# Value projections of 512 columns, and merge gates moved into the attention heads, in a hybrid encoder block

## The chip, the cores and the metric

The kernel runs on one core of a Trainium2 chip. A core has a matrix engine (TensorE, PE in the profile), a vector engine (VectorE, DVE), a scalar engine for activations (ScalarE, ACT), a general engine (GpSimd, POOL) and a queue engine that issues transfers (SyncE, SP). Each runs its own list of instructions in order and waits on semaphores for the others. PE writes to PSUM banks (128 partitions x 512 float32); the other data sits in on-chip SBUF tiles.

The metric is the device time of one execution in microseconds (us), the median of several runs. The profile comes from one further execution; its span runs from the first to the last profiled instruction, and the device time of that execution is a little longer.

## The reference

One block for 512 positions of 1024 features, in float32:

```
u = rmsnorm(x) @ w_in        # columns q | k | v | rnn_x | rnn_gate | gate_A | gate_B, 1024 each
A = chunked_band_attention(q, k, v, rel_table)      # 16 heads x 64, chunks of 64, each with 8 chunks before it
B = rg_lru(conv4(rnn_x)) * gelu(rnn_gate)           # recurrence, 16 block-diagonal gates
gA, gB = sigmoid([gate_A, gate_B] + b_merge)
h = x + (gA * (A @ w_attn_out) + gB * (B @ w_rnn_out)) @ w_o
h = h + (silu(rmsnorm(h) @ w_g) * (rmsnorm(h) @ w_u)) @ w_ffn_out
out = rmsnorm(h)
```

With 512 positions the band of 9 chunks covers every earlier position, so attention is causal by chunk, with a bias per head that depends on the distance (clipped at 128) and a softmax over the keys.

## The kernel before

**Products.** Every large product is made of three matmuls on a rounded high part and a remainder of each operand (`mm3`, lines 76 to 78). The splitting into the two parts (`split`, lines 82 and 83) takes one ScalarE copy for the high part and one VectorE subtraction for the remainder; weights are split the same way after they are loaded. A projection tile is 8 blocks of features x 3 = 24 matmuls into one PSUM bank.

**Weights.** `plan` writes down the order in which weights are used; each has 1024 rows and some columns, loaded as tiles of 512 KB (tag `raw`, three buffers, issued by SP at line 152) and split into tiles tagged `whl` (four buffers of 8 KB a partition in the pool `wp`). `weights(name, ahead)` asks, through `prefetch`, for the named weight and `ahead` further ones. `homes` names another pool for the split tiles of some weights: `v1` to `v3` go to `big` buffers of the pool `rnp`, which the results of the recurrence and later the attention outputs share, and one of them to the later home of two gate tiles.

**Order.** The instructions are put in order when the kernel is built, by a scheduler that walks a simulated time line and takes the program's order as priority; each engine then runs its fixed list. On PE the order inside the attention heads is the program's own (`manual_schedule`).

**First stage** (lines 578 to 588): for four pairs of feature tiles, the projections `xr`, `gr` (recurrent input and its gate), for the first two pairs also `ga` (gate of the attention branch, tiles 0 to 3), and `gb`. Beside them VectorE, ScalarE and GpSimd do the convolution, the GELU, the gates and the scan.

**Between** (lines 629 to 738): queries and keys of the first pair of heads (`q_tile(0)`, `k_tile(0)`), the first four value tiles, and eight tiles `po_yb` of `B @ w_rnn_out`, with the scores of head 0 among them.

**Heads** (lines 739 to 749): for each head h, PE runs in this order: transposes of the probabilities of h (`pT`, line 682), scores of h+1 (`s`, lines 663 and 664), the tiles that `laid(h)` puts before the weighted sum, the weighted sum of h (`o`, line 702), and the tiles that `laid(h)` puts after it. Between the scores of a head and its transposes lies a chain on the other engines: VectorE adds the bias and takes the maximum (line 667), ScalarE takes the exponential with its sum (668), VectorE the reciprocal (669), and GpSimd multiplies (671). `laid` puts `q_tile` or `k_tile` before the sum of heads 0 to 12, one value tile of 256 columns (four heads) behind heads 0 to 11, and the gate tiles 4 to 7 behind head 12 and before the sums of heads 13 to 15. The bias of a head is a broadcast load of 256 KB (`bias_tile`, two buffers, issued by SP at line 430), followed by a `memset` of one corner on GpSimd.

**After** the heads: `ya` = A @ w_attn_out, merge, `w_o`, the feed-forward part and the last norm; the change does not touch them.

Of the kernel before, what the change touches and what calls it, by code (L numbers as in the profile page):

```python
# [8 lines left out]
F32 = mybir.dt.float32  # L9
# [27 lines left out]
def block_kernel(ctx: ExitStack, tc: tile.TileContext, x, norm_mix_g, w_in, b_merge, rel_table,  # L37
# [62 lines left out]
    for j in range(0, KT, 2):  # L100
        plan(f"xr{j}", cols(w_in, C_XR + j * P))
        plan(f"gr{j}", cols(w_in, C_GR + j * P))
        if j < 4:
            plan(f"ga{j}", cols(w_in, C_GA + j * P))
        plan(f"gb{j}", cols(w_in, C_GB + j * P))

    def plan_qk(pr):
        plan(f"qk{pr}", cols(w_in, C_Q + pr * P, P), cols(w_in, C_K + pr * P, P))

    def plan_v(gr):  # L110
        plan(f"v{gr}", cols(w_in, C_V + gr * CW))

    plan_qk(0)
    plan_v(0)
    for j in range(0, KT, 2):
        plan(f"yb{j}", cols(w_rnn_out, j * P))
    for pr in range(1, HEADS // 2):
        plan_qk(pr)
        if pr in (1, 3, 5):
            plan_v((pr + 1) // 2)  # L120
    for j in (4, 6):
        plan(f"ga{j}", cols(w_in, C_GA + j * P))
    for j in range(0, KT, 2):
        plan(f"ya{j}", cols(w_attn_out, j * P))
    for cc in range(2):
# [94 lines left out]
    def prefetch(n):  # L220
        while len(made) < min(n, len(chunks), index.get(barrier[0], len(chunks))):
            name, parts, rows, kts = chunks[len(made)]
            if name in strassen:
                made.append(weight_sums(name))
                continue
            tiles = []
            wide = sum(width for *_, width in parts)
            step = 4 * CW // wide
            for k in range(0, kts, step):
                n_ = min(step, kts - k)  # L230
                if (name, k) in homes:
                    pl, tag, bufs = homes[name, k]
                    hl = pl.tile([P, 2, n_, wide], F32R, tag=tag, bufs=bufs, name=f"whl_{name}_{k}")
                elif name in extra:
                    hl = extra[name].tile([P, 2, n_, wide], F32R, tag="whl", bufs=4, name=f"whl_{name}_{k}")
                else:
                    hl = wp.tile([P, 2, n_, wide], F32R, tag="whl", bufs=4, name=f"whl_{name}_{k}")
                if (name, k) not in raws:
                    load(name, k)
                raw = raws.pop((name, k))  # L240
                if len(made) == 0 and k:
                    act.activation(hl[:, 0], raw[:], AF.Copy)
                    pool.tensor_sub(hl[:, 1], raw[:], f(hl[:, 0]))
                else:
                    split(hl[:, 0], hl[:, 1], raw[:])
                tiles.append(hl)
            made.append(lambda part, k, at, tiles=tiles, step=step: tiles[k // step][:, part, k % step, at])

    def weights(name, ahead=1):
        prefetch(index[name] + 1 + ahead)  # L250
# [175 lines left out]
    def bias_tile(h):  # L426
        b = aw.tile([P, S], F32, tag="bias", bufs=2, name=f"bias{h}")
        src = ext_d[h:h + 1, 0:S]
        band = bass.AP(tensor=src.tensor, offset=src.offset, ap=[[1, P], [1, S]])
        sp.dma_start(out=b[:], in_=band)  # L430
        pool.memset(b[64:128, 448:512], NEG)
        return b

# [131 lines left out]
        return po  # L565


    zs = [[zp.tile([P, 2, S], F32, name=f"z{w}{j}") for j in range(0, KT // (1 + (w == "a")), 2)] for w in "ab"]
    ta, zB = ([t[j // 2][:, j % 2] for j in range(2 * len(t))] for t in zs)
    for gr in (1, 2, 3):  # L570
        for k in (0, 4):
            homes[f"v{gr}", k] = (zp, "late", 1) if (gr, k) == (3, 4) else (rnp, "big", 4)

    def gate(w, j):
        po = tile_of(f"g{'ab'[w]}{j - j % 2}", j % 2)
# [3 lines left out]
    for j in range(0, KT, 2):  # L579
        for c in range(2):  # L580
            conv[j + c] = rnn_conv(j + c, tile_of(f"xr{j}", c, ahead=2))
        for c in range(2):
            po = tile_of(f"gr{j}", c, "mm" if j == 0 else "t")
            conv[j + c] += (rnn_gelu(j + c, po),)
            gates_of(j + c)
        for w in range(j // 4, 2):
            for c in range(2):
                gate(w, j + c)


    rg_stack.close()
# [44 lines left out]

    vs = {}

    def v_tile(gr, t):
        wv = weights(f"v{gr}")  # L640
        po = mm_tile(f"po_v{gr}_{t}", "mm" if gr else "t")
        for k in range(KT):
            mm3(po[:, 0:256], xnT[k][:, 0, t * P:(t + 1) * P], xnT[k][:, 1, t * P:(t + 1) * P],
                wv(0, k, whole), wv(1, k, whole), k == 0, k == KT - 1)
        v = aw.tile([P, 2, 4, HD], F32R, tag="v", bufs=8, name=f"v{gr}_{t}")
        split(v[:, :, 0::3], v[:, :, 1:3], po[:, 0:256].rearrange("p (a b d) -> p a b d", a=2, b=2))
        vs.setdefault(gr, []).append(v)


    def scores(h):  # L650
        pr, e = divmod(h, 2)
        q, kh, kl = qk[pr]
        bias = bias_tile(h)
        lsum = cp.tile([P, NT], F32, tag="lsum", bufs=2, name=f"l{h}")
        nmax = cp.tile([P, NT], F32, tag="nmax", bufs=2, name=f"m{h}")
        rl = cp.tile([P, NT], F32, tag="rl", bufs=2, name=f"rl{h}")
        prob = [aw2.tile([P, (qb + 1) * P], F32, tag=f"p{qb}", name=f"p{h}_{qb}") for qb in range(NT)]
        banks = [ss.tile([P, S], F32, tag="s", bufs=2, name=f"s{h}_{i}") for i in range(2)] + [mm_tile(f"s{h}_2")]
        scs = [banks[0][:, 0:P], banks[0][:, P:3 * P], banks[1][:, 0:3 * P], banks[2][:]]
        for qb in range(NT):  # L660
            w = (qb + 1) * P
            qs = q[:, e, qb * P:(qb + 1) * P]
            pe.matmul(scs[qb], qs, kh[:, e, 0:w], start=True, stop=False)
            pe.matmul(scs[qb], qs, kl[:, e, 0:w], start=False, stop=True)
        for qb in range(NT):
            w = (qb + 1) * P
            dve.tensor_tensor_reduce(prob[qb][:], scs[qb], bias[:, S - w:S], -1.0, 3e38, ALU.add, ALU.min, nmax[:, qb:qb + 1])  # L667
            act.activation(prob[qb][:], prob[qb][:], AF.Exp, bias=nmax[:, qb:qb + 1], scale=-1.0, accum_out=lsum[:, qb:qb + 1])  # L668
        dve.reciprocal(rl[:], lsum[:])  # L669
        for qb in range(NT):  # L670
            pool.tensor_scalar(prob[qb][:], prob[qb][:], rl[:, qb:qb + 1], 1.0, ALU.mult, ALU.mult)  # L671
        return prob
# [18 lines left out]
    def weigh(h, pp):  # L691
        pr, e = divmod(h, 2)
        own, other = halves(e)
        if e == 0:
            oacc.append(tg_.tile([P, S], F32, tag="tg", name=f"oacc{pr}"))
        acc = oacc[pr]
        po = mm_tile(f"o{h}")
        for kb in range(NT):
            i, lo, n = ((0, 0, 512), (1, 0, 384), (2, 0, 256), (2, 256, 128))[kb]
            st = vs[pr // 2][kb][:, pr % 2, 2 * e:2 * e + 2].rearrange("p a d -> p (a d)")  # L700
            for part in range(2):
                pe.matmul(po[:, S - n:S], st, pp[i][:, part, lo:lo + n], start=kb == 0 and part == 0, stop=kb == NT - 1 and part == 1)  # L702
        act.activation(acc[own, :], po[other, :], AF.Copy)
        dve.tensor_add(acc[own, :], po[own, :], acc[own, :])
        if e == 1:
            if pr % 2 == 0:
                aT_pairs.append(rnp.tile([P, 2, 2, S], F32R, tag="big", bufs=4, name=f"aT{pr}"))
            o = aT_pairs[-1][:, pr % 2]
            split(blocks(o[:, 0]), blocks(o[:, 1]), backwards(acc[:]))
            aT.append(o)  # L710

    def laid(h):
        before, after = [], []
        if h == 0:
            before += [lambda: q_tile(1), lambda: k_tile(1)]
        elif h < 13:
            before.append(lambda: (q_tile if h % 2 else k_tile)(1 + (h + 1) // 2 if h % 2 else 1 + h // 2))
        if h < 12:  # L720
            after.append(lambda: v_tile(1 + h // 4, h % 4))
        if h == 12:
            late = zp.tile([P, 2, 2, S], F32, tag="late", bufs=1, name="za_late")
            ta.extend(late[:, i, c] for i in range(2) for c in range(2))
            after.append(lambda: gate(0, 4))
        elif h > 12:
            before.append(lambda: gate(0, h - 8))
        return before, after

    for t in range(NT):  # L730
        v_tile(0, t)
# [7 lines left out]
    with tc.manual_schedule(engines={mybir.EngineType.PE}):  # L739
        for h in range(HEADS):  # L740
            pp = transposed(h, prob)
            if h + 1 < HEADS:
                prob = scores(h + 1)
            before, after = laid(h)
            for what in before:
                what()
            weigh(h, pp)
            for what in after:
                what()
    aw2_stack.close()  # L750
    wo_stack, wop = opened("wo", 4)
    extra["wo1"] = wop
# [253 lines left out]
```

## Time and profile before

| | us |
|---|---|
| device time, three runs | 878.87, 879.03, 879.04 (median 879.03) |
| device time of the profiled execution | 878.95 |
| its span | 877.2 |
| mean granted clock of TensorE | 0.998 |

In the rows of a time line the first number is the start in us from the span's start, the second the duration in us, then engine, line, operation, tile written <- tiles read, shape and count; a bracket gives the idle time of the engine just before, and what ended it. Durations of matmuls overlap, since they are pipelined: what a matmul costs is the distance to the next one's start. The list of issues shows a transfer's queue (SPq, ACTq), size and time to landing.

### The profile page before, as it was taken

What the parts mean: (1) busy time and instruction counts of PE and PEld (TensorE: products, weight loads), DVE (VectorE), ACT (ScalarE), POOL (GpSimd) and SP (SyncE); (2) the same over time, 40 slices, a digit from 0 to 9 for tenths busy, and PEclk for the clock granted to TensorE, in tenths of its full rate; (3) what the DMA queues carried; (4) which work ended last, traced back from release to release, by engine and by line L of the source; (5) the groups of instructions that cost most, each with busy time, mean ns of one, the idle gap of its engine ahead of it and who ended that gap; (6) DMA issues with size and microseconds to landing.
All of it is one profiled execution on the core that took longest, in us unless ns stands there. A gap on an engine that the chain in (4) does not pass through costs nothing.

```text
span 877.2 us, 13330 instructions
## 1 busy us (share of the span) xinstructions
PE 868.0 (99%) x5220; PEld 770.6 (88%) x5220; DVE 544.0 (62%) x858; ACT 483.6 (55%) x838; POOL 105.8 (12%) x138
## 2 busy tenths in 40 slices
PE   8999999999999999999999999999999999999997
PEld 6977888788888899998888889999999999888886
DVE  5776557563466676665556557888888886554203
ACT  6586757752367676666534367555555555723103
POOL 2013112120112232333100000000000001301100
PEclk9999999999999999999999999999999999999999
DMA  8323323333343233222224530433333332353002
GB/s 269 97 78 98 98 87 97 121 96 96 108 138 91 74 93 88 72 73 61 88 85 148 207 96 28 142 101 117 98 103 102 118 112 74 134 177 120 26 1 97
DMA packets 86080, 90.11 MB, mean 103 GB/s; under 512 B 5376, under 2 KB 74608, under 8 KB 86016
## 3 DMA queue, kind: packets, MB, share of 16 engines
q1 hardware_dynamic: 84640, 85.78, 31.5%
q10 hardware_dynamic: 1376, 3.47, 1.0%
q8 instruction: 41, 0.67, 0.3%
q14 instruction: 23, 0.19, 0.1%
HBM read 87.10 MB, written 2.14 MB: 102 GB/s over the span
## 4 chain that ended last, share of the span: by engine, by line
PE 97%; ACT 1%; DVE 1%; DMA 0%; issue 0%; ACTq 0%
PE po_out L76 5%; PE po_out L77 5%; PE po_out L78 5%; PE p_fg L76 2%; PE o L702 2%; PE p_fg L78 2%; PE p_fu L78 2%; PE p_fg L77 2%; PE p_fu L77 2%; PE p_fu L76 2%; PE pT L682 2%; PE po_v L76 2%; PE po_v L78 2%; PE po_v L77 2%; PE po_gb L77 2%; PE po_ga L76 2%
## 5 line engine op out<-in xcount | busy, mean ns | idle before, releaser
L77 PE MATMUL po_out<-whl_fo,act_hi 128*128 128x512 f32 (+1 forms) x198 | 72.5, 366 | 0.0
L76 PE MATMUL po_out<-whl_fo,act_hi 128*128 128x512 f32 (+1 forms) x198 | 72.3, 366 | 0.0
L78 PE MATMUL po_out<-whl_fo,act_lo 128*128 128x512 f32 (+1 forms) x198 | 71.7, 365 | 0.0
L83 DVE TENSOR_TENSOR whl_fo<-raw_fo,whl_fo 128x1024 fp32r<-128x1024 f32 x22 | 27.9, 1274 | 44.2 <-ACT whl_fo L82 43.8
L671 POOL TENSOR_SCALAR p<-p,rl 128x128 f32<-128x128 f32 (+1 forms) x64 | 39.6, 638 | 127.6 <-DVE rl L669 127.3
L82 ACT ACTIVATE whl_fo<-raw_fo 128x1024 fp32r<-128x1024 f32 x22 | 23.1, 1058 | 48.8 <-PE po_out L78 35.2
L890 POOL TENSOR_TENSOR act_lo<-act,act_hi 128x1024 fp32r<-128x1024 f32 x4 | 10.9, 2717 | 323.5 <-ACT act_hi L889 321.5
L668 ACT ACTIVATE p<-p,m 128x128 f32<-128x128 f32 (+1 forms) x64 | 35.8, 560 | 16.2 <-DVE m L667 16.2
L78 PEld LDWEIGHTS po_out<-whl_fo,act_lo 128*128 128x128 f32 x198 | 37.3, 189 | 6.0
L76 PEld LDWEIGHTS po_out<-whl_fo,act_hi 128*128 128x128 f32 x198 | 37.4, 189 | 6.0
L77 PEld LDWEIGHTS po_out<-whl_fo,act_hi 128*128 128x128 f32 x198 | 37.4, 189 | 5.8
L76 PE MATMUL po_v<-whl_v,xnT 128*128 128x256 f32 x128 | 36.8, 287 | 0.0
L78 PE MATMUL po_v<-whl_v,xnT 128*128 128x256 f32 x128 | 36.2, 283 | 0.0
L77 PE MATMUL po_v<-whl_v,xnT 128*128 128x256 f32 x128 | 36.2, 283 | 0.0
L83 DVE TENSOR_TENSOR pp<-pT,pp 128x384 fp32r<-128x384 f32 (+1 forms) x48 | 27.8, 597 | 8.5 <-ACT pp L82 8.5
L667 DVE CUSTOM_DVE_ANT_0 p<-s,bias 128x128 f32<-128x128 f32 (+1 forms) x64 | 29.1, 484 | 0.0
L76 PE MATMUL po_gr<-xnT,whl_gr 128*128 128x512 f32 (+1 forms) x80 | 28.2, 354 | 0.1
L83 DVE TENSOR_TENSOR whl_qk<-raw_qk,whl_qk 128x1024 fp32r<-128x1024 f32 x16 | 21.2, 1326 | 11.0 <-ACT whl_qk L82 11.0
L83 DVE TENSOR_TENSOR whl_fg_s<-s_fg,whl_fg_s 128x1024 fp32r<-128x1024 f32 x20 | 25.6, 1294 | 3.7 <-ACT whl_fg_s L82 3.7
L77 PE MATMUL po_xr<-xnT,whl_xr 128*128 128x512 f32 (+1 forms) x80 | 27.8, 353 | 0.0
L77 PE MATMUL po_gr<-xnT,whl_gr 128*128 128x512 f32 (+1 forms) x80 | 27.6, 346 | 0.0
L78 PE MATMUL po_gr<-xnT,whl_gr 128*128 128x512 f32 (+1 forms) x80 | 27.5, 348 | 0.0
(340 smaller groups left out, 3027.8 us busy)
## 6 DMA issues: line engine op xcount, KB each, us to landing
raw_fg<-in_w_ffn_in_dram SPq DMA_DIRECT2D x24, 512.0 KB, 4.2
raw_fu<-in_w_ffn_in_dram SPq DMA_DIRECT2D x22, 512.0 KB, 4.1
raw_fo<-in_w_ffn_out_dram SPq DMA_DIRECT2D x22, 512.0 KB, 4.0
raw_qk<-in_w_in_dram SPq DMA_DIRECT2D x32, 256.0 KB, 4.0
raw_xr<-in_w_in_dram SPq DMA_DIRECT2D x8, 512.0 KB, 4.6
raw_gr<-in_w_in_dram SPq DMA_DIRECT2D x8, 512.0 KB, 3.4
raw_ga<-in_w_in_dram SPq DMA_DIRECT2D x8, 512.0 KB, 4.0
raw_gb<-in_w_in_dram SPq DMA_DIRECT2D x8, 512.0 KB, 3.5
```

The lines of the kernel that those rows point to most:

```text
L76: pe.matmul(o, sh, mh, start=start, stop=False, skip_group_check=parts)
L77: pe.matmul(o, sh, ml, start=False, stop=False, skip_group_check=parts)
L78: pe.matmul(o, sl, mh, start=False, stop=stop, skip_group_check=parts)
L82: act.activation(hi, src, AF.Copy)
L83: dve.tensor_sub(lo, src, f(hi))
L667: dve.tensor_tensor_reduce(prob[qb][:], scs[qb], bias[:, S - w:S], -1.0, 3e38, ALU.add, ALU.min, nmax[:, qb:qb + 1])
L668: act.activation(prob[qb][:], prob[qb][:], AF.Exp, bias=nmax[:, qb:qb + 1], scale=-1.0, accum_out=lsum[:, qb:qb + 1])
L671: pool.tensor_scalar(prob[qb][:], prob[qb][:], rl[:, qb:qb + 1], 1.0, ALU.mult, ALU.mult)
L682: pe.transpose(pt[:, at * P:(at + 1) * P], prob[qb][:, kb * P:(kb + 1) * P], ident[:])
L702: pe.matmul(po[:, S - n:S], st, pp[i][:, part, lo:lo + n], start=kb == 0 and part == 0, stop=kb == NT - 1 and part == 1)
L890: (pool if i in (0, 1, 2, 4) else dve).tensor_sub(lo[:], o[:], f(hi[:]))
```

## The change

- The value projection is made in tiles of 512 columns (eight heads) in place of 256 (four heads): two weights `v0` and `v1` in place of four, eight tiles in place of sixteen. A value tile has twice the size, in the same eight buffers.
- The gate tiles of the attention branch (`ga`, all eight) are made in the heads, from head 7 on; none is left in the first stage. Their results go to the value buffers that fall free, in place of a tile pool of their own.
- A table `laid` replaces the function: names before the bar stand before the weighted sum, those behind it after. Each tile of keys from pair 1 on has another tile between it and the next head's scores.
- The split weights of `v1` go to three `big` buffers and one `whl`; a home for two tiles of `v0` is set ahead of `v_tile`.
- The bias of head h+1 is asked for with the scores of h, and issued from ScalarE's queue in place of SP's. It keeps two buffers.

```diff
     for j in range(0, KT, 2):
         plan(f"xr{j}", cols(w_in, C_XR + j * P))
         plan(f"gr{j}", cols(w_in, C_GR + j * P))
-        if j < 4:
-            plan(f"ga{j}", cols(w_in, C_GA + j * P))
         plan(f"gb{j}", cols(w_in, C_GB + j * P))
...
     def plan_v(gr):
-        plan(f"v{gr}", cols(w_in, C_V + gr * CW))
+        plan(f"v{gr}", cols(w_in, C_V + gr * S, S))
...
+    def plan_ga(j):
+        plan(f"ga{j}", cols(w_in, C_GA + j * P))
+
     for pr in range(1, HEADS // 2):
         plan_qk(pr)
-        if pr in (1, 3, 5):
-            plan_v((pr + 1) // 2)
-    for j in (4, 6):
-        plan(f"ga{j}", cols(w_in, C_GA + j * P))
+        for at, what, n in ((1, plan_v, 1), (5, plan_ga, 0), (6, plan_ga, 2), (7, plan_ga, 4), (7, plan_ga, 6)):
+            if pr == at:
+                what(n)
...
+                if (name, k) not in raws:
+                    load(name, k)
+                raw = raws.pop((name, k))
                 if (name, k) in homes:
-                    pl, tag, bufs = homes[name, k]
-                    hl = pl.tile([P, 2, n_, wide], F32R, tag=tag, bufs=bufs, name=f"whl_{name}_{k}")
-                elif name in extra:
+                    pl, tag, bufs, each = homes[name, k]
+                    for i in range(0, n_, each):
+                        hl = pl.tile([P, 2, each, wide], F32R, tag=tag, bufs=bufs, name=f"whl_{name}_{k + i}")
+                        split(hl[:, 0], hl[:, 1], raw[:, i:i + each])
+                        tiles.extend((hl, n) for n in range(each))
+                    continue
...
-        sp.dma_start(out=b[:], in_=band)
+        act.dma_start(out=b[:], in_=band)
...
-    zs = [[zp.tile([P, 2, S], F32, name=f"z{w}{j}") for j in range(0, KT // (1 + (w == "a")), 2)] for w in "ab"]
-    ta, zB = ([t[j // 2][:, j % 2] for j in range(2 * len(t))] for t in zs)
-    for gr in (1, 2, 3):
-        for k in (0, 4):
-            homes[f"v{gr}", k] = (zp, "late", 1) if (gr, k) == (3, 4) else (rnp, "big", 4)
+    zs = [zp.tile([P, 2, S], F32, name=f"zb{j}") for j in range(0, KT, 2)]
+    ta, zB = [], [zs[j // 2][:, j % 2] for j in range(KT)]
+    for k in range(0, 6, 2):
+        homes["v1", k] = (rnp, "big", 4, 2)
...
-        for w in range(j // 4, 2):
-            for c in range(2):
-                gate(w, j + c)
+        for c in range(2):
+            gate(1, j + c)
...
+    for k in (4, 6):
+        homes["v0", k] = (aw, "v", 8, 1)
+
...
-            mm3(po[:, 0:256], xnT[k][:, 0, t * P:(t + 1) * P], xnT[k][:, 1, t * P:(t + 1) * P],
-                wv(0, k, whole), wv(1, k, whole), k == 0, k == KT - 1)
-        v = aw.tile([P, 2, 4, HD], F32R, tag="v", bufs=8, name=f"v{gr}_{t}")
-        split(v[:, :, 0::3], v[:, :, 1:3], po[:, 0:256].rearrange("p (a b d) -> p a b d", a=2, b=2))
+            mm3(po[:], xnT[k][:, 0, t * P:(t + 1) * P], xnT[k][:, 1, t * P:(t + 1) * P],
+                wv(0, k, every), wv(1, k, every), k == 0, k == KT - 1)
+        v = aw.tile([P, 4, 4, HD], F32R, tag="v", bufs=8, name=f"v{gr}_{t}")
+        split(v[:, :, 0::3], v[:, :, 1:3], po[:].rearrange("p (a b d) -> p a b d", a=4, b=2))
...
-        bias = bias_tile(h)
+        if not biases:
+            biases.append(bias_tile(0))
+        if h + 1 < HEADS:
+            biases.append(bias_tile(h + 1))
+        bias = biases[h]
...
+    def gate_a(j):
+        if j % 2 == 0:
+            za = aw.tile([P, 2, S], F32, tag="v", bufs=8, name=f"za{j}")
+            ta.extend(za[:, c] for c in range(2))
+        gate(0, j)
+
+    laid = ("q1 k1 | v0", "q2 |", "k2 | v1", "q3 |", "k3 | v2", "q4 v3 |", "k4 | q5", "k5 | g0",
+            "g1 |", "q6 | g2", "k6 | g3", "q7 |", "k7 | g4", "g5 |", "g6 |", "g7 |")
+    kinds = {"q": q_tile, "k": k_tile, "v": lambda t: v_tile(1, t), "g": gate_a}
...
-            before, after = laid(h)
-            for what in before:
-                what()
+            before, after = laid[h].split("|")
+            project_all(before)
             weigh(h, pp)
-            for what in after:
-                what()
+            project_all(after)
```

More of the change, by code (lines that the diff above doesn't have):

```diff
@@ L230, in prefetch @@
                 n_ = min(step, kts - k)
+                if (name, k) not in raws:
+                    load(name, k)
+                raw = raws.pop((name, k))
                 if (name, k) in homes:
-                    pl, tag, bufs = homes[name, k]
-                    hl = pl.tile([P, 2, n_, wide], F32R, tag=tag, bufs=bufs, name=f"whl_{name}_{k}")
-                elif name in extra:
+                    pl, tag, bufs, each = homes[name, k]
[4 more added lines that the diff above has]
+                    continue
+                if name in extra:
                     hl = extra[name].tile([P, 2, n_, wide], F32R, tag="whl", bufs=4, name=f"whl_{name}_{k}")
@@ L237, in prefetch @@
                     hl = wp.tile([P, 2, n_, wide], F32R, tag="whl", bufs=4, name=f"whl_{name}_{k}")
-                if (name, k) not in raws:
-                    load(name, k)
-                raw = raws.pop((name, k))
                 if len(made) == 0 and k:
@@ L245, in prefetch @@
                     split(hl[:, 0], hl[:, 1], raw[:])
-                tiles.append(hl)
-            made.append(lambda part, k, at, tiles=tiles, step=step: tiles[k // step][:, part, k % step, at])
+                tiles.extend((hl, n) for n in range(n_))
+            made.append(lambda part, k, at, tiles=tiles: tiles[k][0][:, part, tiles[k][1], at])
     def weights(name, ahead=1):
@@ L642, in v_tile @@
         for k in range(KT):
-            mm3(po[:, 0:256], xnT[k][:, 0, t * P:(t + 1) * P], xnT[k][:, 1, t * P:(t + 1) * P],
-                wv(0, k, whole), wv(1, k, whole), k == 0, k == KT - 1)
-        v = aw.tile([P, 2, 4, HD], F32R, tag="v", bufs=8, name=f"v{gr}_{t}")
-        split(v[:, :, 0::3], v[:, :, 1:3], po[:, 0:256].rearrange("p (a b d) -> p a b d", a=2, b=2))
+            mm3(po[:], xnT[k][:, 0, t * P:(t + 1) * P], xnT[k][:, 1, t * P:(t + 1) * P],
+                wv(0, k, every), wv(1, k, every), k == 0, k == KT - 1)
+        v = aw.tile([P, 4, 4, HD], F32R, tag="v", bufs=8, name=f"v{gr}_{t}")
+        split(v[:, :, 0::3], v[:, :, 1:3], po[:].rearrange("p (a b d) -> p a b d", a=4, b=2))
         vs.setdefault(gr, []).append(v)
+    biases = []
     def scores(h):
@@ L699, in weigh @@
             i, lo, n = ((0, 0, 512), (1, 0, 384), (2, 0, 256), (2, 256, 128))[kb]
-            st = vs[pr // 2][kb][:, pr % 2, 2 * e:2 * e + 2].rearrange("p a d -> p (a d)")
+            st = vs[pr // 4][kb][:, pr % 4, 2 * e:2 * e + 2].rearrange("p a d -> p (a d)")
             for part in range(2):
@@ L710, in weigh, with project_all @@
             aT.append(o)
[L714 to L728, printed above, removed]
+    def gate_a(j):
[6 more added lines that the diff above has]
+    kinds = {"q": q_tile, "k": k_tile, "v": lambda t: v_tile(1, t), "g": gate_a}
+    def project_all(names):
+        for n in names.split():
+            kinds[n[0]](int(n[1:]))
     for t in range(NT):
```

## The prediction

> **What bounds the kernel now.** I read the page's totals first, then the chain that ended last, then the busy time by stage, and only then the spacing of single matmuls.
>
> ```profile
> span 877.2 us, 13330 instructions
> PE 868.0 (99%) x5220; PEld 770.6 (88%) x5220; DVE 544.0 (62%) x858; ACT 483.6 (55%) x838; POOL 105.8 (12%) x138
> PE 97%; ACT 1%; DVE 1%; DMA 0%; issue 0%; ACTq 0%
> ```
>
> The busy time by stage: a stretch in us and its length, then the busy us of PE, PEld (weight loads), VectorE (DVE), ScalarE (ACT) and GpSimd (POOL) with their instructions, PE's granted clock, and DMA.
>
> ```profile
> 0.00:38.00 38.00, 35.24 (x243) 29.46 (x244) 22.96 (x48) 25.17 (x46) 6.31 (x10) 1.00 0.57 183
> 38.00:178.00 140.00, 140.00 (x627) 111.64 (x627) 87.39 (x119) 97.44 (x128) 26.96 (x24) 1.00 0.32 98
> 178.00:245.00 67.00, 67.00 (x346) 57.52 (x345) 32.98 (x45) 26.28 (x38) 7.62 (x9) 1.00 0.33 100
> 245.00:435.00 190.00, 190.00 (x1131) 169.91 (x1130) 122.03 (x270) 126.34 (x272) 48.00 (x87) 1.00 0.30 86
> ```
>
> TensorE (PE) is busy 99% of the span and makes 97% of the chain. From 38 to 435 us, which holds every tile that the change touches, it is busy for the whole of each stretch (140.00 of 140.00, 67.00 of 67.00, 190.00 of 190.00), at full clock. So there is no stall to remove; time can only come from TensorE's own stream, and only a new stall can cost any. A busy TensorE need not be at its peak, so the stream has to be priced from the starts of its instructions:
>
> ```profile
> 247.11 0.40 PE L76 MATMUL po_q<-xnT,whl_qk 128*128 128x512 f32 x1
> ...
> 252.58 0.39 PE L76 MATMUL po_k<-xnT,whl_qk 128*128 128x512 f32 x1
> ...
> 258.02 0.39 PE L702 MATMUL o<-pp,v 128*128 128x512 f32 x1
> ...
> 259.23 0.33 PE L76 MATMUL po_v<-whl_v,xnT 128*128 128x256 f32 x1
> ...
> 262.15 0.27 PE L682 MATMUL pT<-ident,p 128*128 128x128 f32 x1
> ...
> 402.83 0.44 PE L76 MATMUL po_ga<-xnT,whl_ga 128*128 128x512 f32 x1
> ...
> 408.36 0.27 PE L682 MATMUL pT<-ident,p 128*128 128x128 f32 x1
> ```
>
> Each of these tiles is 24 matmuls. With 512 columns one takes 5.47 us from its start to the next tile's (247.11 to 252.58), 5.44 us where another such tile stands ahead of it (252.58 to 258.02), and 5.53 us where it stands behind a head's weighted sum and ahead of the next transposes (402.83 to 408.36). A value tile of 256 columns takes 2.92 us in that place (259.23 to 262.15). Half the columns take more than half the time: 24 matmuls of 512 are 227 ns each (5.44/24), of 256 some 120 ns (2.92/24 = 122, with the entry).
>
> **The change part by part.**
>
> *Wide value tiles.* Sixteen tiles of 256 columns become eight of 512. Four small ones stand ahead of the heads, the other twelve behind heads 0 to 11:
>
> ```profile
> 188.37 0.28 PE L76 MATMUL po_v<-whl_v,xnT 128*128 128x256 f32 x1
> ...
> 194.12 0.40 PE L76 MATMUL po_yb<-rnn,whl_yb 128*128 128x512 f32 x1
> ```
>
> Two of the four take 5.75 us (188.37 to 194.12), so four take 11.50; twelve take 12 x 2.92 = 35.04; together 46.54. New: four ahead of the heads at 5.44 = 21.76; three behind heads at 5.53 and one behind a tile of queries at 5.44 = 22.03; together 43.79. That is -2.75 us. The evictions (ScalarE, then VectorE) become half as many and about twice as long; they lie beside TensorE.
>
> *Gate tiles moved.* Four gate tiles of the attention branch leave the first stage:
>
> ```profile
> 61.89 0.39 PE L76 MATMUL po_xr<-xnT,whl_xr 128*128 128x512 f32 x1
> ...
> 107.67 0.39 PE L76 MATMUL po_xr<-xnT,whl_xr 128*128 128x512 f32 x1
> ...
> 142.58 0.39 PE L76 MATMUL po_xr<-xnT,whl_xr 128*128 128x512 f32 x1
> ```
>
> A pair of recurrent tiles with gate A takes 45.78 us (61.89 to 107.67), one without it 34.91 (107.67 to 142.58): 10.87 for two gates, 21.74 for four. In the heads three of them stand behind a head at 5.53 and one ahead of the weighted sum at 5.47: 22.06, so +0.32. The queries of pair 5 also move behind a head (5.53 for 5.47): +0.06. The stream's sum is -2.75 + 0.32 + 0.06 = **-2.4 us**.
>
> *What covers the first stage then.* Pairs 2 and 3 already run without gate A, with TensorE busy throughout and the same work per pair on VectorE and ScalarE. Pairs 0 and 1 become like them. Only pair 0 differs: it starts with a VectorE backlog, which already costs something:
>
> ```profile
> 37.16 0.28 PE L78 MATMUL po_gr<-xnT,whl_gr 128*128 128x256 f32 x1
> 37.76 0.47 PE L76 MATMUL po_ga<-xnT,whl_ga 128*128 128x512 f32 x1 [0.33 <-DVE sp_p L453]
> ```
>
> A matmul of 256 columns is followed after 0.60 us instead of 0.12: 0.48 lost. The gate-B tile takes that place, and its weights take the load and conversion slots of the gate-A weights. I count 0; the ends are -0.48 (this gap goes) and +2.76 (all that TensorE idles in the first 38 us, 38.00 less 35.24, comes once more).
>
> *Weights.* The first 512 value columns need four converted tiles where four buffers exist, two of them still held by the first queries and keys. The new `homes["v0", ...]` cannot help: the conversion is asked for by `q_tile(0)`, ahead of the line that sets it. So the third and fourth tile are converted where today the first `w_rnn_out` tiles are, which wait for the same buffers:
>
> ```profile
> 187.92 1.06 ACT L82 ACTIVATE whl_yb<-raw_yb 128x1024 fp32r<-128x1024 f32 x1
> 189.50 1.05 ACT L82 ACTIVATE whl_yb<-raw_yb 128x1024 fp32r<-128x1024 f32 x1
> 190.88 1.21 DVE L83 TENSOR_TENSOR whl_yb<-raw_yb,whl_yb 128x1024 fp32r<-128x1024 f32 x1
> ```
>
> The fourth would be ready at 192.1; the first wide tile starts at 188.4 and comes to it after 18 of 24 matmuls, at 192.5. Cover 0.4 us, cost 0; without the cover about one conversion, 1.2 us.
>
> *Biases.* Two buffers remain, so the bias of head h+1 can still be loaded only once scores h-1 have been read; and the load is already issued then:
>
> ```profile
> SPq L430 <- DVE m L667: 74.3, 13, 11.0
> ...
> 236.66 0.46 SPq L430 DMA_DIRECT2D bias<-ext_d  x1
> ...
> 478.14 1.32 ACTq L773 DMA_DIRECT2D h<-in_x_dram  x3
> 479.52 0.63 ACT L82 ACTIVATE mT<-za_late 128x512 fp32r<-128x512 f32 x1 [0.34 <-DVE za_late L761]
> ```
>
> SP waits 74.3 us in all for that read, with weight loads behind it; no TensorE idle comes of it, so freeing SP gains 0. On ScalarE's queue 16 issues of about 0.4 us (three in 1.32) come between activations, behind each the exponentials and evictions of the head; the wait itself ends with a VectorE instruction that ScalarE's last exponential needs as well. Cost 0 in a long head, up to 0.4 in a short one.
>
> *Short heads.* This is the only place where I expect a cost. Heads 1, 3, 8 and 11 now carry one tile instead of a projection and a value tile; heads 13 and 14 have that shape already. A head begins with its transposes, which need the softmax of the scores made in the head before, normalised on GpSimd (POOL). In head 13:
>
> ```profile
> 410.73 0.39 PE L76 MATMUL po_ga<-xnT,whl_ga 128*128 128x512 f32 x1
> 414.34 3.02 POOL L671 TENSOR_SCALAR p<-p,rl 128x128 f32<-128x128 f32 x4 [7.46 <-DVE rl L669]
> 417.38 0.29 PE L682 MATMUL pT<-ident,p 128*128 128x128 f32 x1
> ...
> 419.77 0.40 PE L76 MATMUL po_ga<-xnT,whl_ga 128*128 128x512 f32 x1
> 424.57 2.05 POOL L671 TENSOR_SCALAR p<-p,rl 128x128 f32<-128x128 f32 x4 [7.21 <-DVE rl L669]
> 426.45 0.30 PE L682 MATMUL pT<-ident,p 128*128 128x128 f32 x1
> ```
>
> Scores end at 410.73, normalising at 417.36, the next transposes start at 417.38: 6.63 us of work in 6.65. Head 14 needs 6.85 (419.77 to 426.62) and loses almost nothing, since the first transposes need only the first blocks. So a short head has no slack but also no stall today. For the four new ones I take the same, plus 0.3 in all (most of one 0.4 us bias issue); the ends are 0 and the rival below.
>
> The sum: 877.2 - 2.4 + 0.3 = 875.1 of span. The profiled execution took 878.95 with that span, 1.75 around it; so 876.8. The median of the three runs shown is 879.03, 0.08 above it, which I neglect.
>
> *A rule that speaks against it.* The Trainium skill (TensorE: Matmul & The Clock Gate, Back-to-back issue gap) puts a warm matmul at N/2.4 + 2.5 ns. As an estimate from that page, 384 x 109.2 ns less 192 x 215.8 ns is only 0.5 us gained. The measured 120 and 227 ns do not follow it at either width.
>
> **The rivals.**
>
> *Late softmax in short heads (slower).* In head 2 the chain is much longer:
>
> ```profile
> 276.48 0.40 PE L76 MATMUL po_k<-xnT,whl_qk 128*128 128x512 f32 x1
> 279.43 1.06 ACT L82 ACTIVATE whl_qk<-raw_qk 128x1024 fp32r<-128x1024 f32 x1 [0.48 <-PE po_k L78]
> 280.53 1.23 DVE L83 TENSOR_TENSOR whl_qk<-raw_qk,whl_qk 128x1024 fp32r<-128x1024 f32 x1 [1.32 <-ACT whl_qk L82]
> 282.61 0.15 POOL L431 MEMSET bias<- 64x64 f32 x1 [11.44 <-DMA bias<-ext_d]
> 282.85 3.02 POOL L671 TENSOR_SCALAR p<-p,rl 128x128 f32<-128x128 f32 x4
> ```
>
> A weight conversion slips ahead of the last exponential and of the reciprocal, the bias's memset waits for its load ahead of the normalising, and that ends at 285.87, 9.39 us after the scores. In a long head this is hidden; in a short one it costs 9.39 - 6.65 = 2.7 us. For it: conversions go wherever an engine has a gap. Against it: this one was freed by a tile of keys in the same head (its releaser is `po_k`), and all tiles of keys now stand in long heads; of the new short ones only head 8 ends the use of a weight. The Trainium skill (SBUF — State Buffer, SBUF: two separate sides) has VectorE with two SBUF inputs and GpSimd lock each other out for a whole instruction; the 3.02 beside 2.05 us of the same four operations agree in sign. One such head (in place of the 0.3) gives 874.8 + 2.7 + 1.75 = 879.25: no change. From two on it decides: 874.8 + 5.4 + 1.75 = 881.95; all four, 887.35.
>
> *First pair starves.* The +2.76 of above: 876.8 + 2.76 = 879.6, no change. For: the backlog of pair 0. Against: gate B and the next pair's projection need no result of pair 0.
>
> *No cost per matmul.* If TensorE's time went by columns alone, halving the matmuls would give nothing and the moves' +0.38 would remain: 878.95 + 0.38 = 879.3, no change. The two spacings speak clearly against it. By the page's gap of above it would be 878.95 - 0.5 + 0.38, about 878.8, as an estimate.
>
> **How the numbers follow.** 0.2% of 879.03, about what a measurement of this kernel can tell from no change, is 1.8 us: faster is below 877.3, slower above 880.8. Forecast 0.55 (its own range 875.8 to 877.3, with the 0.48 gap gone at the low end); one late head 0.15, first pair 0.10 and no cost per matmul 0.04 make 0.29 for no change; two or more late heads 0.16, slower. The range goes from 875.8 to 880.8: what lies above is the 0.16, and little lies below.
>
> **What would show it.** Right: value tiles of 5.44 to 5.53 us; TensorE busy throughout from 38 us to the end of the heads; short heads of about 9.0 us, with normalising ending beside the next transposes; pairs of 34.9 us in the first stage; the heads longer by some 9 us, the stage ahead of them by 10.3, the first shorter by 21.7. Wrong: a TensorE idle with GpSimd's normalising as its releaser in heads 1, 3, 8 or 11; a gap between the first pair's tiles; 512-column tiles above 5.6 us.

## The result and the profile after

The changed kernel takes 877.06 us (median of 12 runs, 876.9 to 877.78) against 879.03 us before (12 runs): a ratio of 0.9977, with a 95% interval of 0.9969 to 0.9984. That is 1.97 us less. By the bound set in the prediction (below 877.3) the median is faster. The interval, 1.4 to 2.7 us less, lies wholly below no change, but it reaches across the 1.8 us of that bound. The forecast was 876.8. The profiled execution took 877.08 with a span of 875.3, so 1.78 around it.

The totals of the page of the changed kernel:

```profile
span 875.3 us, 12954 instructions
PE 864.5 (99%) x5028; PEld 760.0 (87%) x5028; DVE 545.9 (62%) x850; ACT 479.7 (55%) x830; POOL 104.2 (12%) x138
```

There are 192 matmuls fewer (5220 to 5028): eight value tiles of 24 in place of sixteen. TensorE's busy time falls by 3.5 us, and the span by 1.9; 0.9 of the 3.5 lie ahead of the first projection (7.80 us busy there before, 6.87 after), outside what was changed. TensorE remains the bound. Busy time by stage, cut at the new ends of the stages (columns as in the prediction):

```profile
0.00:38.00 38.00, 34.07 (x242) 28.91 (x242) 22.72 (x48) 24.88 (x45) 6.31 (x10) 1.00 0.57 183
38.00:157.00 119.00, 118.93 (x533) 94.28 (x534) 86.47 (x117) 91.18 (x122) 25.70 (x24) 1.00 0.33 98
157.00:235.00 78.00, 78.00 (x355) 64.90 (x354) 36.64 (x47) 29.31 (x41) 6.75 (x9) 1.00 0.35 105
235.00:434.00 199.00, 199.00 (x1028) 170.80 (x1027) 122.69 (x263) 126.46 (x269) 48.54 (x87) 1.00 0.30 87
```

TensorE is again busy for the whole of each stretch from 38 us on. The missing 0.07 of the second one is the tail of a gap at 37.74 to 38.07, which is the gap that the first pair had before. So the change can only be read from the spacing of TensorE's instructions. Its time line, changed kernel: the first pair, the pairs, the queries, the value tiles and the heads.

```profile
9.85 0.50 PE L76 MATMUL po_xr<-xnT,whl_xr 128*128 128x256 f32 x2 [0.19 <-ACT xnT L365]
...
37.46 0.28 PE L78 MATMUL po_gr<-xnT,whl_gr 128*128 128x256 f32 x1
38.07 0.47 PE L76 MATMUL po_gb<-xnT,whl_gb 128*128 128x512 f32 x1 [0.33 <-DVE sp_p L457]
...
86.21 0.39 PE L76 MATMUL po_xr<-xnT,whl_xr 128*128 128x512 f32 x1
...
121.12 0.39 PE L76 MATMUL po_xr<-xnT,whl_xr 128*128 128x512 f32 x1
...
156.02 0.39 PE L76 MATMUL po_q<-xnT,whl_qk 128*128 128x512 f32 x1
...
166.90 0.39 PE L76 MATMUL po_v<-whl_v,xnT 128*128 128x512 f32 x1
...
233.48 0.27 PE L693 MATMUL pT<-ident,p 128*128 128x128 f32 x1
...
247.97 0.44 PE L76 MATMUL po_v<-whl_v,xnT 128*128 128x512 f32 x1
...
253.49 0.27 PE L693 MATMUL pT<-ident,p 128*128 128x128 f32 x1
...
262.51 0.29 PE L693 MATMUL pT<-ident,p 128*128 128x128 f32 x1
...
346.71 0.40 PE L76 MATMUL po_ga<-xnT,whl_ga 128*128 128x512 f32 x1
...
353.39 0.29 PE L693 MATMUL pT<-ident,p 128*128 128x128 f32 x1
...
432.11 0.44 PE L76 MATMUL po_ya<-aT,whl_ya 128*128 128x512 f32 x1
```

The reader sees a pair without gate A in 34.91 us (86.21 to 121.12), a wide value tile behind a head's sum in 5.52 (247.97 to 253.49), and head 1, a short one, in 9.02 (253.49 to 262.51). The gap in the first pair is where it was: 0.61 us between the starts (37.46 to 38.07), now ahead of gate B instead of gate A.

The same stage boundaries before, in TensorE's time line:

```profile
9.54 0.50 PE L76 MATMUL po_xr<-xnT,whl_xr 128*128 128x256 f32 x2 [0.19 <-ACT xnT L361]
...
177.49 0.39 PE L76 MATMUL po_q<-xnT,whl_qk 128*128 128x512 f32 x1
...
244.75 0.27 PE L682 MATMUL pT<-ident,p 128*128 128x128 f32 x1
...
434.27 0.44 PE L76 MATMUL po_ya<-aT,whl_ya 128*128 128x512 f32 x1
```

| stretch | before | after | difference | of it forecast |
|---|---|---|---|---|
| start to first projection | 9.54 | 9.85 | +0.31 | 0 |
| first projection to first queries | 167.95 | 146.17 | -21.78 | -21.74 |
| first queries to first transposes | 67.26 | 77.46 | +10.20 | +10.26 |
| heads | 189.52 | 198.63 | +9.11 | +9.11, and 0.3 for a stall |
| behind the heads | 442.93 | 443.19 | +0.26 | 0 |
| span | 877.2 | 875.3 | -1.9 | -2.1 |

The forecast column is the prediction's own sum set out by stage: 21.76 - 11.50 = 10.26 ahead of the heads, 22.03 - 35.04 + 22.06 + 0.06 = 9.11 in them. The stream (all that TensorE does from the first projection to the end of the heads) came out within 0.1 us in every stage. What missed cancels nearly: no stall in the short heads (0.3 less), but 0.31 more at the start and 0.26 more at the end, both outside everything that the prediction looked at.

The new short heads, by GpSimd's time line of the changed kernel. The first row normalises the probabilities of head 2, whose scores are made in the short head 1; the last one those of head 9, whose scores are made in the short head 8:

```profile
259.49 2.05 POOL L682 TENSOR_SCALAR p<-p,rl 128x128 f32<-128x128 f32 x4 [7.42 <-DVE rl L680]
261.60 0.15 POOL L435 MEMSET bias<- 64x64 f32 x1
...
350.33 3.01 POOL L682 TENSOR_SCALAR p<-p,rl 128x128 f32<-128x128 f32 x4 [7.46 <-DVE rl L680]
```

In short head 1 the normalising ends at 261.54 and the next transposes start at 262.51: 0.97 us to spare. In short head 8 it ends at 353.34 and the transposes start at 353.39, 0.05 to spare, which is the least of the four; heads 3 and 11 have 0.97 and 0.37. The memset of the next bias comes behind the normalising, not ahead of it as in head 2 before. No short head waited.

### The profile page after: what moved, and what is told of

Read it like the earlier page. It is cut to its first block, busy times and chain, and to the rows that moved or that the text cites. A ratio compares the mean times of both kernels' runs of the same rounds, so it can differ in the third digit from the quotient of the medians.

```text
span 875.3 us, 12954 instructions
## 1 busy us (share of the span) xinstructions
PE 864.5 (99%) x5028; PEld 760.0 (87%) x5028; DVE 545.9 (62%) x850; ACT 479.7 (55%) x830; POOL 104.2 (12%) x138
## 4 chain that ended last, share of the span: by engine, by line
PE 97%; ACT 1%; DVE 1%; DMA 0%; issue 0%; ACTq 0%
PE po_out L76 5%; PE po_out L78 5%; PE po_out L77 5%; PE p_fg L76 2%; PE o L713 2%; PE p_fg L77 2%; PE p_fg L78 2%; PE p_fu L78 2%; PE p_fu L77 2%; PE p_fu L76 2%; PE pT L693 2%; PE po_gb L77 2%; PE po_gb L76 2%; PE po_ga L76 2%; PE po_v L76 2%; PE po_ga L78 2%
## 5 line engine op out<-in xcount | busy, mean ns | idle before, releaser
L77 PE MATMUL po_xr<-xnT,whl_xr 128*128 128x512 f32 (+1 forms) x80 | 27.9, 354 | 0.0
L78 PE MATMUL po_xr<-xnT,whl_xr 128*128 128x512 f32 (+1 forms) x80 | 27.3, 346 | 0.0
L76 PE MATMUL po_xr<-xnT,whl_xr 128*128 128x512 f32 (+1 forms) x80 | 26.6, 351 | 0.6 <-ACT xnT L365 0.6
L83 DVE TENSOR_TENSOR whl_fu_s<-s_fu,whl_fu_s 128x1024 fp32r<-128x1024 f32 x20 | 24.0, 1220 | 4.5 <-ACT whl_fu_s L82 4.5
```

The source lines that it names most:

```text
L76: pe.matmul(o, sh, mh, start=start, stop=False, skip_group_check=parts)
L77: pe.matmul(o, sh, ml, start=False, stop=False, skip_group_check=parts)
L78: pe.matmul(o, sl, mh, start=False, stop=stop, skip_group_check=parts)
L83: dve.tensor_sub(lo, src, f(hi))
```

## The experiments

Each was timed in turn with the kernel before on one chip; 879.0 us stands for it throughout (878.95 with value halves, quarters, the bias part undone and one tile of keys, 878.97 with the other four). The changed kernel was run with the second four only (876.93); differences of the first four to its 877.06 hold to about 0.1 us, by which the kernel before differs between the series. The diffs are against the changed kernel.

### One part undone: value tiles as two halves

```diff
+        for at in (slice(i, i + 256) for i in range(0, S, 256)):
             for k in range(KT):
-            mm3(po[:], ..., wv(0, k, every), wv(1, k, every), ...)
+                mm3(po[:, at], ..., wv(0, k, at), wv(1, k, at), ...)
```

> The changed kernel, with each 512-column value tile made as two halves of 256 columns one after the other in the same PSUM bank (192 matmuls of 512 columns become 384 of 256); everything else stays. Theory (the gain is TensorE's own stream: 24 matmuls of 256 columns take 2.88 us, of 512 columns 5.44 to 5.53): eight tiles take 5.76 in place of 5.47, +2.4 us over the changed kernel, so 0.4 us above the kernel before, about 879.4. Rival (the gain comes from the gates that were moved, the order of the heads or the bias loads): as the changed kernel, about 877.1.

Measured: 879.45 us, ratio to before 1.001 (1.0001 to 1.0019), 2.39 more than the changed kernel, with runs scattered from 879.12 to 881.61. In its time line a value tile takes 5.81 us (248.88 to 254.69):

```profile
248.88 0.33 PE L76 MATMUL po_v<-whl_v,xnT 128*128 128x256 f32 x1
...
254.69 0.27 PE L694 MATMUL pT<-ident,p 128*128 128x128 f32 x1
```

Eight tiles at 5.81 - 5.52 = 0.29 make 2.3 us, and the run gives back all of the gain. The weights, their transfers and conversions, the evictions and the order are those of the changed kernel. What doubles is the number of matmuls, each with the load of its own 128x128 operand into TensorE. So the gain comes from the width of the matmul and not from fewer evictions, moved gates or bias loads. The trace also shows the rest of the change by itself: from the first projection to the end of the heads it takes 424.76 us, against 424.73 before and 422.26 in the changed kernel. Without the width nothing is left of the gain there. The moved tiles' 0.38 was not run alone, and cannot be told apart in this sum from the eight tiles fewer.

### The same cost doubled: four quarters

The same edit with 128 in place of 256.

> The same with four quarters of 128 columns (768 matmuls of 128 columns for the values). Two models of what a matmul costs besides its columns: a constant 13 ns on top of N/2.4 (227 ns at 512, 120 at 256) gives 66 ns at 128 columns, so 768 x 66 - 192 x 227 = +7 us over the changed kernel, about 884; a floor of about 110 ns under every matmul that loads new weights (the 109 ns between transposes) gives 768 x 110 - 192 x 227 = +41 us, about 918.

Measured: 918.87 us, 1.0456 (1.0442 to 1.0471), 41.8 more than the changed kernel. The time line, in a value tile:

```profile
170.09 0.28 PE L78 MATMUL po_v<-whl_v,xnT 128*128 128x128 f32 x1
170.21 0.27 PE L76 MATMUL po_v<-whl_v,xnT 128*128 128x128 f32 x1
170.32 0.28 PE L77 MATMUL po_v<-whl_v,xnT 128*128 128x128 f32 x1
...
170.99 0.28 PE L77 MATMUL po_v<-whl_v,xnT 128*128 128x128 f32 x1
```

These stand some 0.112 us apart (eight steps from 170.09 to 170.99): a matmul of 128 columns costs nearly what one of 256 does (0.12), and half of one of 512 (0.227). With 768 matmuls at 0.112 in place of 192 at 0.227 the sum is +42.4, close to the 41.8 measured. From 512 to 256 columns the cost falls by 107 ns, from 256 to 128 by some 8 only: the second of the two models in the expectation, a floor of about 110 ns, is the one that holds.

### The bias part undone

```diff
-        act.dma_start(out=b[:], in_=band)
+        sp.dma_start(out=b[:], in_=band)
...
-        if not biases:
-            biases.append(bias_tile(0))
-        if h + 1 < HEADS:
-            biases.append(bias_tile(h + 1))
-        bias = biases[h]
+        bias = bias_tile(h)
```

> The changed kernel with the bias loads as before: issued by SP, and asked for with the head's own scores. Theory (two buffers let the load start no earlier either way, and TensorE waits for no bias): no change against the changed kernel, within 0.3 us, about 877.1. Rival (the short heads need the early load): each of the six short heads loses up to 1 us to the memset ahead of the normalising, 880 to 883.

Measured: 876.56 us, 0.9973 (0.9963 to 0.9983), 0.5 less than the changed kernel. Heads and stage ahead of them are unchanged: in its time line the first queries, the first transposes and the first tile behind the heads stand at 155.84, 233.30 and 431.92 us, 77.46 and 198.62 apart, to 0.01 as in the changed kernel. Loading the biases early gains nothing, as forecast, and the short heads hold without it. The 0.5 us (0.37 against the 876.93 of the same kernel below) are more than the 0.3 that the expectation allowed, and they are not in the heads: 0.17 of them lie at the start (the first projection stands at 9.68 us in place of 9.85), and 0.31 behind the last tile of the heads. Two runs follow that up.

### The changed kernel once more, and the queue alone

The second of these leaves the early request and only puts the load back on SP's queue (the first two lines of the diff above).

> The changed kernel itself, beside the next three on one chip, so that differences of some tenths can be read: about 877.1 (0.9977 of the kernel before).

> The changed kernel with one word changed: the bias loads are issued by SP, but still asked for one head early. Undoing queue and early request together left 0.5 us less (876.56). In the profiles 0.3 us of that lies behind the last matmul, between the last output transfer's issue and the end, and 0.2 ahead of the first projection. Theory (the queue does it: the end is later where ScalarE's queue carries the bias loads; the start is chance): 0.3 us less than the changed kernel in the same call, with an end 5.9 to 6.0 us behind the last matmul in place of 6.3. Rival (the early request does it, or it is chance): as the changed kernel.

Measured: the changed kernel again 876.93 (0.9975, 0.9966 to 0.9984); with SP's queue 876.59 (0.9973, 0.9962 to 0.9983), the time of the run before. The last output transfer's issue, in the time lines of the kernel before, the changed one and the one with SP's queue:

```profile
873.47 0.35 ACTq L952 DMA_DIRECT2D out_dram<-h  x1
```

```profile
871.29 0.35 ACTq L959 DMA_DIRECT2D out_dram<-h  x1
```

```profile
871.07 0.35 ACTq L959 DMA_DIRECT2D out_dram<-h  x1
```

From the end of this issue to the end of the span (877.2, 875.3, 874.7) it takes 3.38, 3.66 and 3.28 us. All ten traces divide in this way: 3.62 to 3.69 us in the six with the bias loads on ScalarE's queue, 3.27 to 3.38 in the four with them on SP's, the kernel before among these. So the 0.3 us behind the last work come with the 16 bias loads on ScalarE's queue, over 400 us earlier in the program; it is the queue and not the early request. Why is open (below). The start does not follow the queue: the first projection stands at 9.41 to 9.95 us in the six, with 9.85 and 9.73 in two runs of the changed kernel, and at 9.54 to 9.68 in the four. It is put down to chance here.

### One tile of keys in a short head

```diff
-    laid = ("q1 k1 | v0", "q2 |", "k2 | v1", "q3 |", "k3 | v2", ...
+    laid = ("q1 k1 | v0", "q2 |", "k2 |", "q3 | v1", "k3 | v2", ...
```

Head 2, with the keys of pair 2, becomes short, and head 3 long. This tries the rival of the late softmax: keys in a short head, with the weight conversion that they set free.

> The changed kernel with one tile moved by one head: value tile 1 stands behind the queries of pair 3 (head 3) in place of behind the keys of pair 2 (head 2). Head 2 becomes short and its tile of keys has nothing behind it; the scores that need these keys come 2.2 us after the tile. Theory (the eviction of a tile of keys takes about 5 us, and a weight conversion freed by it delays the softmax): one stall of 2.7 to 3.5 us at head 3, about 880.2. Rival (scheduling makes room for the eviction): no stall, 877.1.

Measured: 877.78 us, 0.9989 (0.998 to 0.9998), 0.7 to 0.85 above the changed kernel (877.06 and 876.93) where the rival's price for one head was 2.7. Neither the 2.7 to 3.5 us of the expectation came out nor the absence of a stall that its rival stood for. Heads 2 and 3 take 9.07 and 15.40 us in its trace against 14.60 and 9.02, 0.85 in all. The softmax was not much late: the weight conversion stands behind the last exponential here (268.27 and 267.55), as it does in the changed kernel's own head 2 (268.33 and 267.61), not ahead of it as before the change; and the normalising ends 7.04 us after the scores (264.84 to 271.88) where the rival had 9.39. Most of the loss is one wait ahead of the scores:

```profile
273.33 0.33 PE L674 MATMUL s<-kh,q 128*128 128x128 f32 x1 [0.41 <-ACT kh L627]
```

The scores of head 4 need the keys that were made just ahead of them, and wait for ScalarE's eviction of these. They start 1.81 us after the head's first transposes (271.52), where the changed kernel has 1.01 (277.11 to 278.12). So the tile that the change puts behind each tile of keys hides this wait, some 0.8 us here.

### Keys in short heads behind the middle

```diff
-    laid = (..., "k4 | q5", "k5 | g0",
-            "g1 |", "q6 | g2", "k6 | g3", "q7 |", "k7 | g4", "g5 |", "g6 |", "g7 |")
+    laid = (..., "k4 | q5", "k5 |",
+            "q6 |", "k6 |", "q7 | g0", "k7 | g1", "g2 | g3", "g4 | g5", "g6 |", "g7 |")
```

(The weights of all gate tiles are planned behind the last keys.) Heads 7, 8 and 9 are then short in a row; 7 and 9 hold keys and become short by this edit, 8 was short already. From two late heads on, the prediction had said, the rival decides.

> The changed kernel with the same 26 tiles dealt otherwise from head 7 on: the keys of pairs 5 and 6 stand alone in heads 7 and 9, which become short, and two gate tiles each stand in heads 12 and 13. The next scores that need these keys are two heads away, so only the softmax chain can be late. Rival of the prediction (a weight conversion freed by the keys slips ahead of the softmax, which ends 9.4 us after the scores as in head 2 of the kernel before, with 6.65 available): 2.7 us in each of heads 7 and 9, 5.4 us over the changed kernel, about 882.5. Other theory (what was late in head 2 came from the value tile's eviction, two conversions and the bias's memset at the head's start, not from the keys): normalising 6.6 to 7.0 us after the scores, no change, 877.1.

Measured: 879.19 us, 1.0002 (0.9994 to 1.0011), 2.26 more than the changed kernel in the same series (876.93): neither the rival's 5.4 nor nothing. The heads 8, 9 and 10 take 9.62, 10.20 and 15.16 us, against 9.05 for the changed kernel's short heads and 14.60 for its long ones: 0.57, 1.15 and 0.56 more. All engines in head 8 and at the start of head 9:

```profile
339.48 1.49 DVE L83 TENSOR_TENSOR whl_qk<-raw_qk,whl_qk 128x1024 fp32r<-128x1024 f32 x1 [0.26 <-ACT whl_qk L82]
341.00 0.69 DVE L715 TENSOR_TENSOR oacc<-o,oacc 64x512 f32<-64x512 f32 x1
...
341.75 0.50 PE L76 MATMUL po_q<-xnT,whl_qk 128*128 128x512 f32 x1 [0.28 <-DVE oacc L715]
...
344.50 0.33 ACTq L434 DMA_DIRECT2D bias<-ext_d  x1
...
346.35 0.17 DVE L680 RECIPROCAL rl<-l 128x4 f32<-128x4 f32 x1
...
347.60 0.15 POOL L435 MEMSET bias<- 64x64 f32 x1 [3.35 <-DMA bias<-ext_d]
347.84 2.06 POOL L682 TENSOR_SCALAR p<-p,rl 128x128 f32<-128x128 f32 x4
...
349.29 0.33 PE L693 MATMUL pT<-ident,p 128*128 128x128 f32 x1 [0.23 <-POOL p L682]
```

At head 9 the rival's chain is seen at work, with other parts. A bias load is issued at 344.50; its memset waits for the load and stands ahead of the normalising on GpSimd, which so starts 1.3 us after the reciprocal is ready (346.52 to 347.84). The reciprocal itself is late too: it is ready 4.8 us after the start of the tile behind the scores (341.75 to 346.52), where in the changed kernel's head 8 the normalising has already begun after 3.6 (346.71 to 350.33). The transposes then wait for it block by block. The bias loads are on ScalarE's queue here; the same order with SP's queue was not run. The loss of head 8 comes in another way, in the first rows: the tile of queries waits for the PSUM bank from which VectorE accumulates the outputs (`oacc`), and that stands on VectorE behind a conversion that follows the tile of keys in head 7. Head 10, behind the keys of head 9, loses its 0.56 us to the same wait.

### A version faster than both

The biases as before the change, and the first gate-B tile in the PSUM bank tag `t` in place of `mm`, whose banks the VectorE backlog of the first pair holds.

```diff
-        po = tile_of(f"g{'ab'[w]}{j - j % 2}", j % 2)
+        po = tile_of(f"g{'ab'[w]}{j - j % 2}", j % 2, "t" if (w, j) == (1, 0) else "mm")
```

> The changed kernel with the biases as before (SP, with the head's own scores) and the first gate-B tile in a bank of the other PSUM group, so that it need not wait until the convolution has read its bank. Theory (the gap of 0.60 us ahead of that tile is this bank): the gap falls to the ordinary 0.12, 0.5 us less than with the biases undone alone, 876.1. Rival (the tile waits for its converted weights as well): the gap stays, 876.6.

Measured: 876.0 us, 0.9966 (0.9953 to 0.9978), the fastest. Its time line, and its busy time by stage:

```profile
37.20 0.28 PE L78 MATMUL po_gr<-xnT,whl_gr 128*128 128x256 f32 x1
37.32 0.40 PE L76 MATMUL po_gb<-xnT,whl_gb 128*128 128x512 f32 x1
```

```profile
38.00:156.00 118.00, 118.00 (x530) 93.46 (x529) 83.78 (x115) 89.69 (x120) 25.56 (x24) 1.00 0.32 99
```

The gate-B tile follows after 0.12 us instead of 0.61. The run is 0.59 below the one with only the queue put back (876.59, runs of 876.36 to 876.85 against 875.82 to 876.2); the early request, by which the two also differ, was worth nothing above (876.56 without it, 876.59 with it). The wait in the first pair was one for a bank: the weights of the tile were ready without it.

## Why the prediction was right

**The stream (-2.4 us): right.** From the first projection to the end of the heads it is -21.78 + 10.20 + 9.11 = -2.47. Two small value tiles of 24 matmuls of 256 columns become one of 24 of 512; that step carries it, and the two halves took 2.39 of it back.

**No cost per matmul: fallen.** The trace of before gave 120 and 227 ns; the halves and quarters confirm that the time goes by the matmuls and their width, not by the columns alone. By the rule of the Trainium skill (TensorE: Matmul & The Clock Gate, Back-to-back issue gap), a matmul of 128 columns would take some 56 ns, as an estimate, and by that section's figure for a stream with weight loads 81; measured are some 112.

**First stage (0): right.** The 0.48 gap stayed, as taken, and no other came. The low end of that term, the gap going, was within reach only by another bank, as the last experiment shows. The rival of a starving first pair fell: there is one gap, of 0.61 us between two starts, as before (0.60). Its price was high, too: of the 2.76 us that TensorE idles in the first 38, only 0.70 lay behind the first projection (27.20 of 27.90 us busy from 9.54 to 37.44), and it is 0.69 now (27.20 of 27.89, 9.85 to 37.74).

**Value weights: right.** The home set ahead of `v_tile` does nothing, as forecast: it would cut the conversions of the third and fourth tile into 128x512, and all eight conversions of value weights in the trace are 128x1024. The fourth is converted somewhat earlier than the prediction put it, ready 2.5 us after the first wide tile starts instead of 3.7. ScalarE and VectorE in the changed kernel's time line:

```profile
167.10 1.06 ACT L82 ACTIVATE whl_v<-raw_v 128x1024 fp32r<-128x1024 f32 x1 [0.50 <-PE po_k L78]
168.20 1.23 DVE L83 TENSOR_TENSOR whl_v<-raw_v,whl_v 128x1024 fp32r<-128x1024 f32 x1 [0.33 <-ACT whl_v L82]
```

The fourth is ready at 169.43 and needed after 18 matmuls, at 166.90 + 18 x 0.227 = 171.0: cover 1.6 us, where 0.4 was forecast.

**Biases (0 gained): right in the heads, too small at the end.** SP's freed time brought nothing: with the loads back on SP's queue the kernel is some 0.3 us faster, with the early request (876.59) as without it (876.56). The prediction put the price of ScalarE's issues into the short heads, up to 0.4 each. It is nothing there, and some 0.3 us behind the last work, for which the prediction had no term.

**Short heads (+0.3): 0.** In the tightest of the four the normalising ends 6.63 us after the scores (346.71 to 353.34) and 6.68 are there (to 353.39): "no slack but also no stall" holds, and the bias issue that the 0.3 stood for costs nothing there. The others had 0.37 to 0.97 to spare.

**The late softmax (2.7 us a head): fallen as priced, right as a mechanism.** It took the 9.39 us of head 2 before as what keys cost in a short head. One such head costs 0.7 to 0.85, mostly by the eviction of the keys. Two such heads close together cost 2.26, about 1.15 of it by normalising late behind a bias's memset, the rest by waits for a PSUM bank. The changed kernel has none of this; that this is so because all keys stand in long heads, as the prediction argued, fits both runs, in which keys in short heads cost something each time.

That 877.06 lies so near 876.8 owes something to luck: 0.3 of stall that did not come stands against 0.3 at the end, and 0.3 of a late start in the profiled run.

## What to carry to other kernels

Where an engine is busy throughout, price an edit by the distance between the starts of its instructions at each width, and take both widths from the trace: 24 matmuls saved per wide tile were worth 0.3 us, while going down to 128 columns cost 42 in all. Put a tile that depends on nothing between a projection and the step that reads it: here it hides a wait of 0.8 us for an eviction. Which short stages hold depended here on the work that stood beside them on the other engines, not on their length alone. Look at the start and the end of the span too; a load put on another queue was felt behind the last output.

## What the runs showed of the hardware that was not expected

A matmul of this kernel, with the load of its own 128x128 operand, costs 227 ns at 512 columns, 120 at 256 and some 112 at 128. No run separates the matmul from that load, so what sets the floor at about 110 ns stays open.

With 16 broadcast loads on ScalarE's queue rather than SP's, the program ends about 0.3 us later behind its last issue (3.66 us against 3.38 before and 3.28 with the queue put back, and the same division in all ten traces), though the biases are long loaded by then. The cause was not found.
